# Fixed buffer turns, stores in halves, and a start in half chunks for a matrix product with a decayed running sum

## The chip, the cores and the metric

The kernel runs on one core of a Trainium2 chip. The metric is device time in microseconds (us) of one execution. Times of a kernel are medians of several executions. The profile shows one execution; its span leaves out some 2 us of that execution's time (957.6 of 959.52 us in before).

Engines: TensorE (PE) multiplies, VectorE (DVE) scans and transposes, ScalarE (ACT) reads PSUM and scales, GpSimd (POOL) adds and issues loads, SyncE (SP) issues stores.

## The reference

```python
# x: 16 x 2048 x 1024, w: 1024 x 1024, decay: 1024, all fp32
xw = x @ w
out[:, 0, :] = xw[:, 0, :]
for t in range(1, S):
    out[:, t, :] = decay[None, :] * out[:, t - 1, :] + xw[:, t, :]
```

## The kernel before

The sequence is cut into 64 chunks of 512 steps. GpSimd loads a chunk of x as bf16, VectorE transposes it ("turn"), and VectorE or ScalarE copies it into the layout for the product ("part"). The result comes in eight column tiles n = 0 to 7 of 128 channels. Most of the time two chunks form a group, and a column tile of a group fills two PSUM banks. A few groups have one chunk; there two column tiles share a two-bank PSUM tile. Of chunk 0, the first six column tiles (the "heads") are multiplied side by side while w arrives. Cut, comment added:

```python
groups = ([[0], [1, 2], [3]] + [[c, c + 1] for c in range(4, nch - 2, 2)]
          + [[nch - 2], [nch - 1]])
...
if len(g) == 2:
    ps = psp.tile([128, T], FP32, name="ps")        # pool of 3
else:
    if gi == 0 and n < 6:
        both = heads[n // 2]
    elif n % 2 == 0:
        both = psp.tile([128, 2, TL], FP32, name="ps")
    ps = both[:, n % 2]
```

A column tile is scanned in one of two ways. A *direct* one is scanned by VectorE from PSUM, over all steps. A *paired* one is read by ScalarE (a copy and a scaled copy of every second step), GpSimd adds the two, and VectorE scans only half as many elements; ScalarE and GpSimd then fill in the other half. VectorE transposes each result back into an output tile, which SyncE stores, in the last chunk together with ScalarE:

```python
def store(self, n0, n1):
    for q in (0, 2, 1, 3):
        queue = nc.scalar if self.final and q >= 2 else nc.sync
        queue.dma_start(out=..., in_=self.ot[quad(q), :, n0 * P:n1 * P])
```

Nearly every instruction is wrapped in `pin(...)`, which holds it behind the earlier ones of its own engine. The stores are not. A compiler pass places what is free.

## Time and profile before

| | before |
|---|---|
| median | 961.5 us |
| span of the profile | 957.6 us |
| TensorE busy | 93% |
| matmuls of 512 columns | 4096 |
| first matmul starts | 15.5 us |
| last matmul ends | 939.1 us |
| last transpose ends | 941.6 us |
| last store lands | 956.7 us |

The page gives a span, busy shares, and rows of 40 slices with a digit for tenths; PEclk is the clock that TensorE was granted, in tenths of full speed. The timeline gives, for each run of like instructions, the start, the length, the engine, the line of the kernel, the operation, the operands, the count, and in brackets the idle time before it and what ended it. The lines themselves are in the prediction.

### The profile page before, as it was taken

What the parts mean: (1) busy time and instruction counts of PE and PEld (TensorE: products, weight loads), DVE (VectorE), ACT (ScalarE), POOL (GpSimd) and SP (SyncE); (2) the same over time, 40 slices, a digit from 0 to 9 for tenths busy, and PEclk for the clock granted to TensorE, in tenths of its full rate; (3) what the DMA queues carried; (4) which work ended last, traced back from release to release, by engine and by line L of the source; (5) the groups of instructions that cost most, each with busy time, mean ns of one, the idle gap of its engine ahead of it and who ended that gap; (6) DMA issues with size and microseconds to landing.
All of it is one profiled execution on the core that took longest, in us unless ns stands there. A gap on an engine that the chain in (4) does not pass through costs nothing.

```text
span 957.6 us, 11691 instructions
## 1 busy us (share of the span) xinstructions
PE 891.8 (93%) x4096; PEld 401.9 (42%) x4096; DVE 828.7 (87%) x617; ACT 687.5 (72%) x969; POOL 662.5 (69%) x768
## 2 busy tenths in 40 slices
PE   3497999999999999999999999999999999999871
PEld 1143444444444444444444444444444444444330
DVE  2579799999999999999999999999999999998872
ACT  2567778777877787787778777877777787776630
POOL 7657677777777777777777777767777776765520
PEclk9699999999999999999999999999999999999997
DMA  9998999999999999999999999999999999995917
GB/s 154 152 169 145 257 177 239 222 232 233 231 220 228 231 218 236 235 235 219 230 220 224 239 231 237 224 226 220 227 235 228 237 226 228 222 228 148 236 55 175
DMA packets 278715, 204.20 MB, mean 213 GB/s; under 512 B 7808, under 2 KB 278144, under 8 KB 278656
## 3 DMA queue, kind: packets, MB, share of 16 engines
q1 hardware_dynamic: 140608, 133.18, 54.9%
q0 software_dynamic: 135936, 69.22, 53.1%
q10 hardware_dynamic: 2112, 1.05, 0.5%
q8 instruction: 32, 0.52, 0.2%
q14 instruction: 27, 0.22, 0.1%
HBM read 138.42 MB, written 134.22 MB: 285 GB/s over the span
## 4 chain that ended last, share of the span: by engine, by line
PE 88%; POOL 3%; issue 2%; DVE 2%; DMA 1%; ACT 1%; DVEq 0%; ACTq 0%; POOLq 0%
PE ps L133 88%; POOL xb L105 1%; DMA xb<-in_x_dram 1%; DVE so L194 1%; DVE ot L214 1%; POOL ot L88 1%; POOL xs L179 0%; ACT xs L173 0%; DVE so L185 0%; ACT h L163 0%; POOL so L207 0%; DVE xw L113 0%; ACT xt L121 0%; DVEq L355 0%; POOL so L176 0%
## 5 line engine op out<-in xcount | busy, mean ns | idle before, releaser
L133 PE MATMUL ps<-xt,wsb 128*128 128x512 bf16 x4096 | 891.8, 381 | 47.4 <-ACT h L163 26.1
L133 PEld LDWEIGHTS <-wsb 128*128 128x128 bf16 x4096 | 401.9, 98 | 536.8 <-issue 42.8
L179 POOL TENSOR_TENSOR xs<-h,xs 128x512 f32<-128x512 f32 (+1 forms) x198 | 246.6, 1246 | 221.4 <-ACT h L163 100.8
L173 ACT COPY xs<-ps 128x1024 f32<-128x1024 f32 (+1 forms) x198 | 193.1, 975 | 179.6 <-PE ps L133 178.0
L214 DVE STREAM_TRANSPOSE ot<-so 128x1024 f32<-128x1024 f32 (+1 forms) x272 | 304.3, 1154 | 2.4 <-POOL so L207 1.0
L207 POOL TENSOR_TENSOR so<-h,xs 128x512 f32<-128x512 f32 (+1 forms) x198 | 245.4, 1240 | 29.0 <-ACT h L163 16.1
L121 ACT COPY xt<-xw 128x2048 bf16<-128x2048 bf16 x126 | 239.7, 1902 | 19.3 <-DVE xw L113 19.3
L105 POOL DMA_DIRECT2D xb<-in_x_dram x256 | 170.3, 666 | 2.0 <-DVE xw L113 1.1
L163 ACT ACTIVATE h<-so,dec 128x512 f32<-128x512 f32 (+1 forms) x198 | 148.9, 752 | 27.0 <-DVE so L185 23.2
L185 DVE TENSOR_TENSOR_SCAN so<-dec,keep,xs 128x512 f32<-128x512 f32 (+1 forms) x102 | 124.3, 1218 | 41.3 <-POOL xs L179 41.0
L113 DVE STREAM_TRANSPOSE xw<-xb 128x2048 f32<-128x2048 f32 x64 | 146.3, 2286 | 9.9 <-DMA xb<-in_x_dram 9.9
L185 DVE TENSOR_TENSOR_SCAN so<-dec,xs 128x512 f32<-128x512 f32 (+1 forms) x96 | 114.4, 1191 | 40.5 <-POOL xs L179 37.2
L163 ACT ACTIVATE h<-ps,dec 128x512 f32<-128x512 f32 (+1 forms) x198 | 133.2, 673 | 0.0
L194 DVE TENSOR_TENSOR_SCAN so<-dec,keep,ps 128x1024 f32<-128x1024 f32 (+1 forms) x42 | 84.8, 2019 | 5.4 <-PE ps L133 4.6
L194 DVE TENSOR_TENSOR_SCAN so<-dec,ps 128x1024 f32<-128x1024 f32 (+1 forms) x32 | 70.2, 2194 | 1.7 <-PE ps L133 1.7
L210 ACT COPY keep<-so 128x1 f32<-128x1 f32 x144 | 26.9, 187 | 1.6 <-DVE so L194 1.6
L178 ACT COPY so<-keep 128x1 f32<-128x1 f32 x102 | 19.5, 191 | 0.0
L88 POOL DMA_DIRECT2D ot<-in_w_dram x16 | 8.8, 552 | 4.8 <-DMA xb<-in_x_dram 4.2
L176 POOL MEMSET so<- 128x1 f32 x96 | 11.2, 117 | 0.0
L245 DVE COPY wsb<-ot 128x1024 bf16<-128x1024 bf16 x6 | 2.6, 462 | 4.4 <-DMA ot<-in_w_dram 4.4
L239 DVE TENSOR_TENSOR dec<-dec 128x8 f32<-128x8 f32 x1 | 0.2, 176 | 7.1 <-DMA dec<-in_decay_dram 7.1
L245 ACT COPY wsb<-ot 128x1024 bf16<-128x1024 bf16 x2 | 2.1, 1045 | 4.7 <-DMA ot<-in_w_dram 4.7
(6 smaller groups left out, 4.1 us busy)
## 6 DMA issues: line engine op xcount, KB each, us to landing
out_dram<-ot SPq DMA_DIRECT2D x116, 1024.0 KB, 15.4
xb<-in_x_dram POOLq DMA_DIRECT2D x256, 256.0 KB, 10.0
out_dram<-ot SPq DMA_DIRECT2D x16, 512.0 KB, 8.0
out_dram<-ot SPq DMA_DIRECT2D x12, 256.0 KB, 4.1
ot<-in_w_dram POOLq DMA_DIRECT2D x16, 128.0 KB, 4.8
out_dram<-ot ACTq DMA_DIRECT2D x4, 256.0 KB, 3.5
dec<-in_decay_dram SPq DMA_DIRECT2D x4, 1.0 KB, 3.1
```

Of the source, the lines that this page charges most:

```text
L105: pin(nc.gpsimd.dma_start(out=xb_of[c][quad(q)], in_=_ap(x, [[D, P], [P * D, NJ], [1, CQ]], (b * S + t0) * D + q * CQ)))
L113: pin(nc.vector.transpose(out=dst.rearrange("p (m j i) -> p j m i", m=M, i=P), in_=src.rearrange("p (j m c) -> p j m c", m=M, c=P)))
L121: pin(copy(out=xt_of[c][:, m0:m1], in_=xw_of[c][:, m0:m1].rearrange("p m t e -> p m e t")))
L133: pin(nc.tensor.matmul(out=ps, lhsT=wsb[:, k, n].rearrange("p q i -> p (q i)"), rhs=xt[:, k // 2, k % 2], start=(k == 0), stop=(k == K - 1),))
L163: pin(nc.scalar.activation(out=h, in_=src, func=mybir.ActivationFunctionType.Copy, scale=dec[:, self.n:self.n + 1]))
L173: pin(nc.scalar.copy(out=self.xs, in_=self.ps))
L179: pin(nc.gpsimd.tensor_tensor(out=self.xs[:, 1:T:2], in0=g, in1=self.xs[:, 1:T:2], op=ALU.add))
L185: pin(nc.vector.tensor_tensor_scan(out=so[:, 3:T + 2:2], data0=dec2[:, n:n + 1].to_broadcast([128, T // 2]), data1=self.xs[:, 1:T:2], init ...
L194: pin(nc.vector.tensor_tensor_scan(out=so[:, 2:T + 2], data0=dec[:, n:n + 1].to_broadcast([128, T]), data1=self.ps, initial=0.0 if self.pr ...
L207: pin(nc.gpsimd.tensor_tensor(out=so[:, 2:T + 2:2], in0=h, in1=self.xs[:, 0:T:2], op=ALU.add))
L210: pin(nc.scalar.copy(out=self.keep, in_=so[:, T + 1:T + 2]))
L214: pin(nc.vector.transpose(out=self.ot[:, :, n * P:(n + 1) * P], in_=self.so[:, 2:T + 2].rearrange("p (i t) -> p i t", t=P)))
```

## The change

Its intent: buffers are named and taken in a fixed turn, not from a pool; stores are pinned, and each group goes out in halves of four column tiles; the first two chunks enter in half chunks, with TensorE fed zeros meanwhile so that its clock is up, and the heads are seven. The order of the groups changes too ([0], [1], then pairs), and so does the set of paired tiles in one-chunk groups. Core of the diff, cuts marked, some comments added:

```diff
-    PAIRED = (0, 1, 2, 4, 5, 6)
+    HEADS = 7
+    def ring(pool, name, count, shape, dtype=FP32):
+        i = turns[name] = turns.get(name, -1) + 1
+        return pool.tile(shape, dtype, name=f"{name}{i % count}")
...
-    groups = ([[0], [1, 2], [3]] + [[c, c + 1] for c in range(4, nch - 2, 2)]
+    groups = ([[0], [1]] + [[c, c + 1] for c in range(2, nch - 2, 2)]
               + [[nch - 2], [nch - 1]])
...
+            if len(g) == 2:
+                self.paired = n % 4 != 3
+            else:
+                self.paired = n % 2 == 0 and not (self.final and n == K - 2)
...
-            if self.halved:
-                if n == K // 2 - 1:
-                    self.store(0, K // 2)
-                elif n == K - 1:
-                    self.store(K // 2, K)
-            elif n == K - 1:
-                self.store(0, K)
+            if n == 3:
+                self.store(0, 4)
+            elif n == 5 and self.final:
+                self.store(4, 6)
+            elif n == 7:
+                self.store(6 if self.final else 4, 8)
...
-                queue.dma_start(
+                pin(queue.dma_start(
...
+    for _ in range(40):
+        pin(nc.tensor.matmul(out=spare, lhsT=idle[:, 0:128], rhs=idle, start=True, stop=True))
+    H = NJ // 2
+    for j0 in (0, H):
+        for q in range(NQ):
+            load(0, q, j0, j0 + H)
...
+    at(1, turn, 1, 0, H)                      # chunk 1: first half behind tile 1 of chunk 0
+    at(1, part, 1, nc.vector.tensor_copy, 0, 2, 0, H)
+    at(1, part, 1, nc.scalar.copy, 2, M, 0, H)
+    at(3, turn_last_half, 1)                  # second half behind tile 3
...
+        elif gi == 1:                         # chunk 1's first four tiles, in halves
+            bank = [ring(psp, "ps", 3, [128, 2, TL]) for _ in range(2)]
+            heads = [bank[n // 2][:, n % 2] for n in range(4)]
+            for t0 in (0, H * P):
+                for n in range(4):
+                    for k in range(K):
+                        matmul(heads[n], n, k, xt_of[1], t0, t0 + H * P)
```

More of the change, by code (lines that the diff above doesn't have):

```diff
@@ L59 @@
     NC = S // TL
-    PAIRED = (0, 1, 2, 4, 5, 6)
+    HEADS = 7
     const = ctx.enter_context(tc.tile_pool(name="const", bufs=1))
-    xbp = ctx.enter_context(tc.tile_pool(name="xbp", bufs=3))
-    xwp = ctx.enter_context(tc.tile_pool(name="xwp", bufs=2))
-    xtp = ctx.enter_context(tc.tile_pool(name="xtp", bufs=5))
-    sop = ctx.enter_context(tc.tile_pool(name="sop", bufs=4))
-    tmp = ctx.enter_context(tc.tile_pool(name="tmp", bufs=2))
-    otp = ctx.enter_context(tc.tile_pool(name="otp", bufs=2))
@@ L69 @@
-    psp = ctx.enter_context(tc.tile_pool(name="psp", bufs=3, space=bass.MemoryType.PSUM))
-    pdp = ctx.enter_context(tc.tile_pool(name="pdp", bufs=1, space=bass.MemoryType.PSUM))
+    sb = ctx.enter_context(tc.tile_pool(name="sb", bufs=1))
+    psp = ctx.enter_context(tc.tile_pool(name="psp", bufs=1, space=bass.MemoryType.PSUM))
+    turns = {}
+    def ring(pool, name, count, shape, dtype=FP32):
+        i = turns[name] = turns.get(name, -1) + 1
+        return pool.tile(shape, dtype, name=f"{name}{i % count}")
@@ L72, in quad @@
     def quad(q):
         return slice(q * P, (q + 1) * P)
-    dec = const.tile([128, K], FP32, name="dec")
-    dec2 = pdp.tile([128, 512], FP32, name="dec2")
-    wsb = const.tile([128, K, K, NQ, P], BF16, name="wsb")
-    with nc.allow_non_contiguous_dma(reason="a vector of 1024"):
-        for q in range(NQ):
-            nc.sync.dma_start(
-                out=dec[quad(q), :], in_=_ap(decay, [[1, P], [P, K]], q * CQ))
-    def load_w():
-        wb = otp.tile([128, M, 2 * D], BF16, name="ot")
-        for m in range(M):
-            for q in range(NQ):
-                pin(nc.gpsimd.dma_start(
-                    out=wb[quad(q), m],
-                    in_=_ap(w, [[2 * D, P], [1, 2 * D]], (q * CQ + m * 2 * P) * D)))
-        return wb.rearrange("p m (e q n i) -> p (m e) q n i", e=2, q=NQ, n=K)
@@ L93 @@
     chunks = [(b, c * TL) for b in range(B) for c in range(NC)]
     nch = len(chunks)
-    xt_of = {}
-    xw_of = {}
-    xb_of = {}
-    def load(c, q):
-        if c >= nch:
-            return
-        b, t0 = chunks[c]
-        if q == 0:
-            xb_of[c] = xbp.tile([128, NJ, CQ], BF16, name="xb")
-        pin(nc.gpsimd.dma_start(
-            out=xb_of[c][quad(q)],
-            in_=_ap(x, [[D, P], [P * D, NJ], [1, CQ]], (b * S + t0) * D + q * CQ)))
-    def turn(c):
-        xw = xwp.tile([128, M, TL, 2], BF16, name="xw")
-        src = xb_of.pop(c).rearrange("p j c -> p (j c)").bitcast(FP32)
-        dst = xw.rearrange("p m t e -> p (m t e)").bitcast(FP32)
-        pin(nc.vector.transpose(
-            out=dst.rearrange("p (m j i) -> p j m i", m=M, i=P),
-            in_=src.rearrange("p (j m c) -> p j m c", m=M, c=P)))
-        xw_of[c] = xw
@@ L118, in part @@
-    def part(c, copy, m0, m1):
-        if m0 == 0:
-            xt_of[c] = xtp.tile([128, M, 2, TL], BF16, name="xt")
-        pin(copy(
-            out=xt_of[c][:, m0:m1],
-            in_=xw_of[c][:, m0:m1].rearrange("p m t e -> p m e t")))
-    groups = ([[0], [1, 2], [3]] + [[c, c + 1] for c in range(4, nch - 2, 2)]
+    groups = ([[0], [1]] + [[c, c + 1] for c in range(2, nch - 2, 2)]
               + [[nch - 2], [nch - 1]])
@@ L128, with ot_tile, load, turn @@
         assert chunks[g[0]][0] == chunks[g[-1]][0]
-    last = {}
-    def matmul(ps, n, k, xt):
+    dec = const.tile([128, K], FP32, name="dec")
+    dec2 = psp.tile([128, 512], FP32, name="dec2")
+    spare = psp.tile([128, TL], FP32, name="spare")
+    wsb = const.tile([128, K, K, NQ, P], BF16, name="wsb")
+    def ot_tile():
+        return ring(sb, "ot", 2, [128, 2 * NJ, CQ])
+    xb_of = {}
+    xw_of = {}
+    xt_of = {}
+    def load(c, q, j0=0, j1=NJ):
+        b, t0 = chunks[c]
+        if c not in xb_of:
+            xb_of[c] = ring(sb, "xb", 3, [128, NJ, CQ], BF16)
+        pin(nc.gpsimd.dma_start(
+            out=xb_of[c][quad(q), j0:j1],
+            in_=_ap(x, [[D, P], [P * D, j1 - j0], [1, CQ]],
+                    (b * S + t0 + j0 * P) * D + q * CQ)))
+    def turn(c, j0=0, j1=NJ):
+        if c not in xw_of:
+            xw_of[c] = ring(sb, "xw", 2, [128, M, NJ, P, 2], BF16)
+        src = xb_of[c][:, j0:j1].rearrange("p j c -> p (j c)").bitcast(FP32)
+        dst = xw_of[c].rearrange("p m j i e -> p (m j i e)").bitcast(FP32)
+        pin(nc.vector.transpose(
+            out=dst.rearrange("p (m j i) -> p j m i", m=M, i=P)[:, j0:j1],
+            in_=src.rearrange("p (j m c) -> p j m c", m=M, c=P)))
+    def part(c, copy, m0, m1, j0=0, j1=NJ):
+        if c not in xt_of:
+            xt_of[c] = ring(sb, "xt", 5, [128, M, 2, TL], BF16)
+        src = xw_of[c][:, m0:m1, j0:j1].rearrange("p m j i e -> p m e (j i)")
+        pin(copy(out=xt_of[c][:, m0:m1, :, j0 * P:j1 * P], in_=src))
+    def matmul(ps, n, k, xt, t0=0, t1=TL):
         pin(nc.tensor.matmul(
-            out=ps,
+            out=ps[:, t0:t1],
             lhsT=wsb[:, k, n].rearrange("p q i -> p (q i)"),
-            rhs=xt[:, k // 2, k % 2],
+            rhs=xt[:, k // 2, k % 2, t0:t1],
             start=(k == 0),
@@ L139, in matmul @@
         ))
+    last = {}
     class Tile:
@@ L150, in __init__ @@
             self.final = gi + 1 == len(groups)
-            self.halved = gi + 3 >= len(groups)
-            self.paired = n in PAIRED and not self.final
-            self.so = sop.tile([128, self.T + 2], FP32, name="so")
+            if len(g) == 2:
+                self.paired = n % 4 != 3
+            else:
+                self.paired = n % 2 == 0 and not (self.final and n == K - 2)
+            self.so = ring(sb, "so", 4, [128, 2 * TL + 2])
             self.prev = None if self.t0 == 0 else last[n]
@@ L161, in decayed @@
         def decayed(self, src):
-            h = tmp.tile([128, self.T // 2], FP32, name="h", bufs=4)
+            h = ring(sb, "h", 4, [128, TL])[:, 0:self.T // 2]
             pin(nc.scalar.activation(
@@ L171, in pair @@
             T = self.T
-            self.xs = tmp.tile([128, T], FP32, name="xs", bufs=3)
+            self.xs = ring(sb, "xs", 3, [128, 2 * TL])[:, 0:T]
             pin(nc.scalar.copy(out=self.xs, in_=self.ps))
@@ L227, in store @@
                 queue = nc.scalar if self.final and q >= 2 else nc.sync
-                queue.dma_start(
+                pin(queue.dma_start(
                     out=_ap(out, [[D, P], [P * D, self.T // P], [1, (n1 - n0) * P]],
                             (self.b * S + self.t0) * D + q * CQ + n0 * P),
-                    in_=self.ot[quad(q), :, n0 * P:n1 * P])
-    for q in range(NQ):
-        load(0, q)
-    wv = load_w()
-    for c in range(1, 3):
-        for q in range(NQ):
-            load(c, q)
+                    in_=self.ot[quad(q), :, n0 * P:n1 * P]))
@@ new lines @@
+    with nc.allow_non_contiguous_dma(reason="a vector of 1024"):
+        for q in range(NQ):
+            nc.sync.dma_start(
+                out=dec[quad(q), :], in_=_ap(decay, [[1, P], [P, K]], q * CQ))
+    idle = const.tile([128, TL], BF16, name="idle")
+    pin(nc.vector.memset(idle, 0.0))
+    for _ in range(40):
+        pin(nc.tensor.matmul(out=spare, lhsT=idle[:, 0:128], rhs=idle, start=True, stop=True))
+    H = NJ // 2
+    for j0 in (0, H):
+        for q in range(NQ):
+            load(0, q, j0, j0 + H)
@@ new lines @@
+    wb = ot_tile().rearrange("p j c -> p (j c)")[:, 0:M * D].bitcast(BF16)
+    wm = wb.rearrange("p (m d) -> p m d", m=M)
+    for m in range(M):
+        for q in range(NQ):
+            pin(nc.gpsimd.dma_start(
+                out=wm[quad(q), m],
+                in_=_ap(w, [[2 * D, P], [1, 2 * D]], (q * CQ + m * 2 * P) * D)))
+    for j0 in (0, H):
+        for q in range(NQ):
+            load(1, q, j0, j0 + H)
+    for q in range(NQ):
+        load(2, q)
+    for j0 in (0, H):
+        turn(0, j0, j0 + H)
+        part(0, nc.vector.tensor_copy, 0, 2, j0, j0 + H)
+        part(0, nc.scalar.copy, 2, M, j0, j0 + H)
@@ L239 @@
     pin(nc.vector.tensor_tensor(out=dec2[:, 0:K], in0=dec, in1=dec, op=ALU.mult))
-    turn(0)
-    part(0, nc.vector.tensor_copy, 0, 2)
-    part(0, nc.scalar.copy, 2, M)
+    wk = wb.rearrange("p (k q n i) -> p k q n i", k=K, q=NQ, n=K)
     for k in range(K):
         copy = nc.scalar.copy if k % 4 == 3 else nc.vector.tensor_copy
-        pin(copy(out=wsb[:, k].rearrange("p n q i -> p q n i"), in_=wv[:, k]))
+        pin(copy(out=wsb[:, k].rearrange("p n q i -> p q n i"), in_=wk[:, k]))
+    agenda = {}
@@ L246, with at @@
     loads = []
-    agenda = {}
-    def prepare(c, l, first):
-        def turned():
-            turn(c)
-            loads.extend((c + 3, q) for q in range(NQ))
-        ahead = (7, 6, 4) if l else (11, 10, 8)
-        steps = (turned, lambda: part(c, nc.scalar.copy, 0, 2),
-                 lambda: part(c, nc.scalar.copy, 2, M))
-        for a, f in zip(ahead, steps):
-            agenda.setdefault(first - a, []).append(f)
+    def at(step, f, *args):
+        agenda.setdefault(step, []).append(lambda: f(*args))
@@ L261, with turn_and_load, turn_last_half @@
+    def turn_and_load(c):
+        turn(c)
+        if c + 3 < nch:
+            loads.extend((c + 3, q) for q in range(NQ))
+    def turn_last_half(c):
+        turn(c, H, NJ)
+        loads.extend((c + 3, q) for q in range(NQ))
+    at(1, turn, 1, 0, H)
+    at(1, part, 1, nc.vector.tensor_copy, 0, 2, 0, H)
+    at(1, part, 1, nc.scalar.copy, 2, M, 0, H)
+    at(3, turn_last_half, 1)
+    at(3, part, 1, nc.vector.tensor_copy, 0, 2, H, NJ)
+    at(3, part, 1, nc.scalar.copy, 2, M, H, NJ)
     for gi, g in enumerate(groups):
@@ L263 @@
             if c > 1:
-                prepare(c, l if len(g) == 2 else 1, gi * K)
-    loads.extend((3, q) for q in range(NQ))
-    turn(1)
-    loads.extend((4, q) for q in range(NQ))
-    part(1, nc.vector.tensor_copy, 0, 2)
-    part(1, nc.scalar.copy, 2, M)
-    def feed(step):
-        for f in agenda.pop(step, []):
-            f()
-        for _ in range(2 if len(loads) > NQ else 1):
-            if loads:
-                load(*loads.pop(0))
+                first = gi * K
+                ahead = (7, 6, 4) if l or len(g) == 1 else (11, 10, 8)
+                at(first - ahead[0], turn_and_load, c)
+                at(first - ahead[1], part, c, nc.scalar.copy, 0, 2)
+                at(first - ahead[2], part, c, nc.scalar.copy, 2, M)
     waiting = []
@@ L297, in behind @@
                 tl.back()
+    loads.extend((3, q) for q in range(NQ))
     for gi, g in enumerate(groups):
@@ L301 @@
         if len(g) == 2:
-            ot = otp.tile([128, T // P, CQ], FP32, name="ot")
+            ot = ot_tile()
         else:
             if g[0] in (0, nch - 2):
-                halves = otp.tile([128, 2 * TL // P, CQ], FP32, name="ot")
+                halves = ot_tile()
             ot = halves[:, g[0] % 2 * NJ:(g[0] % 2 + 1) * NJ]
-        xts = [xt_of.pop(c) for c in g]
+        heads = []
         if gi == 0:
-            heads = [psp.tile([128, 2, TL], FP32, name="ps") for _ in range(3)]
+            bank = [ring(psp, "ps", 3, [128, 2, TL]) for _ in range(3)]
+            heads = [bank[n // 2][:, n % 2] for n in range(6)] + [spare]
@@ L310 @@
             for k in range(K):
-                for n in range(6):
-                    matmul(heads[n // 2][:, n % 2], n, k, xts[0])
+                for n in range(HEADS):
+                    matmul(heads[n], n, k, xt_of[0])
+        elif gi == 1:
[5 more added lines that the diff above has]
+                        matmul(heads[n], n, k, xt_of[1], t0, t0 + H * P)
@@ L313 @@
         for n in range(K):
-            if len(g) == 2:
-                ps = psp.tile([128, T], FP32, name="ps")
-            else:
-                if gi == 0 and n < 6:
-                    both = heads[n // 2]
-                elif n % 2 == 0:
-                    both = psp.tile([128, 2, TL], FP32, name="ps")
-                ps = both[:, n % 2]
-            if gi > 0 or n >= 6:
+            if n < len(heads):
+                ps = heads[n]
+            else:
+                if len(g) == 2:
+                    ps = ring(psp, "ps", 3, [128, T])
+                elif gi == 0:
+                    ps = ring(psp, "ps", 3, [128, 2, TL])[:, 0]
+                else:
+                    if n % 2 == 0:
+                        both = ring(psp, "ps", 3, [128, 2, TL])
+                    ps = both[:, n % 2]
@@ L323 @@
                 for k in range(K):
-                    for l in range(len(g)):
-                        matmul(ps[:, l * TL:(l + 1) * TL], n, k, xts[l])
+                    for l, c in enumerate(g):
+                        matmul(ps[:, l * TL:(l + 1) * TL], n, k, xt_of[c])
             behind(Tile(gi, n, ps, ot))
-            feed(gi * K + n)
+            for f in agenda.pop(gi * K + n, []):
+                f()
+            for _ in range(2 if len(loads) > NQ else 1):
+                if loads:
+                    load(*loads.pop(0))
```

## The prediction

> **What bounds the kernel now.** I read the page's slices first, then the chain that ended last, then the timeline of TensorE at both ends.
>
> ```profile
> PE   3497999999999999999999999999999999999871
> PEclk9699999999999999999999999999999999999997
> 95.41 799.62 PE ps L133 x3704
> ```
>
> The third line is a piece of the chain: start, length, what. For 800 us the chain is nothing but matmuls, 799.62 / 3704 = 0.2159 us each. All 4096 would take 884.3 us; the span is 957.6, so 73 us can be won, and only before 95 us and after 898 us. The timeline of TensorE there (start, length, and in brackets the idle time before and who ended it):
>
> ```profile
> 15.47 12.13 PE L133 MATMUL ps<-xt,wsb 128*128 128x512 bf16 x48 [15.47 <-DVE wsb L245]
> 33.69 3.57 PE L133 MATMUL ps<-xt,wsb 128*128 128x512 bf16 x8 [6.09 <-ACT h L163]
> 45.35 33.26 PE L133 MATMUL ps<-xt,wsb 128*128 128x512 bf16 x144 [8.09 <-ACT h L163]
> ...
> 901.25 3.61 PE L133 MATMUL ps<-xt,wsb 128*128 128x512 bf16 x16 [1.05 <-ACT h L163]
> 907.09 3.61 PE L133 MATMUL ps<-xt,wsb 128*128 128x512 bf16 x16 [2.22 <-ACT h L163]
> ...
> 922.04 3.61 PE L133 MATMUL ps<-xt,wsb 128*128 128x512 bf16 x16 [1.48 <-DVE so L194]
> ...
> 937.23 1.89 PE L133 MATMUL ps<-xt,wsb 128*128 128x512 bf16 x8 [1.41 <-DVE so L194]
> ```
>
> **Start.** At 95.41 us TensorE has done 248 matmuls, worth 53.5 us: 41.9 us lost. 15.5 is data; 6.1 and 8.1 follow; 2.3 goes in the clock, since matmuls come 0.43 us apart at 15.5 and 45.4; the four stops of the one-chunk group [3] cost 6.
>
> **One-chunk groups.** Every stop lies ahead of an odd column tile n: n and n-1 share a two-bank PSUM tile, and the odd half is not written until the even half has been read (n=0 of chunk 62 ends at 900.2, ScalarE reads it until 901.2, n=1 starts at 901.25).
>
> **End.** VectorE ends at 941.6, the span at 957.6. SyncE's queue says why (total wait, times, longest):
>
> ```profile
> SPq L228 <- DMA out_dram<-ot: 32.2, 4, 25.2
> ```
>
> The instruction list shows the stores of chunk 62, ready at about 913 and 922, issued at 935.9 and later. They wait for semaphores that the last chunk's stores on ScalarE's queue had been given first (issued 932.79 and 941.66). The scheduler was free to order the stores. SyncE's last eight stores then go out 944.7 to 951.7, the last landing at 956.7.
>
> **What the Trainium skill says.**
> 1. "TensorE: Matmul & The Clock Gate", Part 1 (the HAM clock gate): an idle array runs at half rate, returns to full after a busy window of about 3.4 us, and falls back after an idle one. The trace agrees: 0.43 against 0.216 us, full rate 3.3 us after 15.47, and half rate again from 32.4.
> 2. "DMA: Bandwidth & Descriptors", Specifications: pieces under 512 B pay a read-modify-write. Stores of halves have 512 B rows, the last four column tiles of the last chunk 256 B rows. The trace has 512 B: queue q1 was busy 92.3% of 16 engines over 904 to 911 us with 3374 packets, 30.6 ns each; the 1 KB packets of 400 to 500 us took 59.2% with 14929, 63.4 ns each. So halves cost the same per byte. No 256 B store is in the trace.
>
> **The change, part by part.**
>
> *Fixed rotation:* in the steady 800 us nothing waits but TensorE, which stopped once. 0 us.
>
> *Stores in halves:* twice the stores, same transfer time (above). 0 us in the middle.
>
> *Spin-up:* 40 matmuls of zeros from about 1 us: some 12 at 0.43 and 28 at 0.216, done by about 12, before data. Half chunks let VectorE turn the first half while the second lands (chunk 0 all landed at 11.4, w in pieces from 13.9 to 21.4, the same bytes in the same order): half turn 1.15 + half copy 0.62 ends at 13.3, then the first piece of w, copied at 14.4, instead of 15.47. With seven heads 56 matmuls take 12.1: TensorE is done at 26.5 (before: 48 at 27.4). One us earlier, eight matmuls more: worth 2.6 us.
>
> *Then the start is bound by VectorE and ScalarE, in fixed order.* Per two column tiles of 512, VectorE does a paired scan 0.62, a direct scan 1.12, two transposes 1.24 (start to start in the trace): 2.98. A turn of a chunk is 2.2. ScalarE needs 1.0 to read a paired tile, POOL 0.7 to add; half of a chunk's copy takes ScalarE 1.9. The timelines of these engines show it (the next start gives the step):
>
> ```profile
> 38.39 0.69 DVE L185 TENSOR_TENSOR_SCAN so<-dec,xs 128x256 f32<-128x256 f32 x1 [0.69 <-POOL xs L179]
> 39.00 1.19 DVE L194 TENSOR_TENSOR_SCAN so<-dec,ps 128x512 f32<-128x512 f32 x1
> 40.11 0.68 DVE L214 STREAM_TRANSPOSE ot<-so 128x512 f32<-128x512 f32 x1
> ...
> 40.88 1.90 ACT L121 COPY xt<-xw 128x2048 bf16<-128x2048 bf16 x1
> 42.68 0.59 ACT L173 COPY xs<-ps 128x512 f32<-128x512 f32 x1
> 43.16 0.49 ACT L163 ACTIVATE h<-ps,dec 128x256 f32<-128x256 f32 x1
> ```
>  Following the program's order on each queue, since nearly every instruction is held to it:
> - n=0 is read by 26.4, POOL adds by 27.2, scans 0 and 1 end at 28.95: n=7 of chunk 0 may then use their banks, 28.95 to 30.7.
> - half turn and copy of chunk 1, ScalarE's copy to 31.15, read of n=2 to 32.1, add 32.8, scans 2 and 3 to 34.6: chunk 1's n=0,1 start on half data.
> - the second half turn and copy to 36.4, read of n=4 37.8, scans 4 and 5 to 40.3: n=2,3 start, and the second half runs to about 45.6.
> - turn of chunk 2 to 42.5; scans 6, 7 to 45.5: n=4 of chunk 1 from 45.6 to 47.3.
> - n=5 needs n=4 read. ScalarE first does two chunk copies (to 47.9), reads n=2, waits for chunk 3's turn (50.7), copies (52.6): n=4 read at 54.2.
> - after 7 us idle the clock is low: n=5 to 57.7, n=6 to 60.3, read 61.3, n=7 to 63.1.
>
> Pairs start at 63.1 with 128 matmuls (27.6 us) done: 35.5 lost, against 41.9. **Start gains 6.4 us.**
>
> *Chunk 62:* n=3 still waits for ScalarE, which waits for VectorE's backlog of 1024-wide transposes and the turn of chunk 63; redoing the list gives n=7 at 917.15 against 916.94 (old clock). 0 us.
>
> *Last chunk:* even tiles are now read by ScalarE in 1.05 instead of VectorE's 1.28 plus what lies ahead of it: a step of two tiles goes from 5.09 to 4.7, three times; n=6 stays direct. VectorE's last transpose ends near 940.6 instead of 941.6. Gain 1.0.
>
> *Last stores:* issued in program order, chunk 62's are out of the way by 930. The last eight (n=4,5 and n=6,7) are 512 packets of 256 B each. I take 30 ns a packet as for 512 B: 0.96 us each over 16 engines. The first four are issued at 937.4, start 1.9 later and end at 943.3; the last four follow to 947.2. The drain after the last landing is 0.95: 948.1 against 957.6. **The end gains 9.5 us, the 1.0 included.**
>
> Sum: 6.4 + 9.5 = 15.9; a little off because the list above leaves out the 20 to 50 ns between a release and the next start, some 30 times on the chain over both ends, and part of that is in the durations: 15.5. Median 961.8 - 15.5 = **946.3 us**.
>
> **Rivals.**
> 1. *The wait moves, not goes, at the start.* If ScalarE's copies hold n=4's read longer, or the clock falls in the idle stretches at 31 and 36 too, the start gains nothing. For: I count 20 us idle of TensorE after 26.5, all by in-order queues. Against: the old start had the same kind of waits, plus the group [3]. Time: 952.
> 2. *The 256 B stores pay the read-modify-write and take 60 ns.* Eight of them take 15.4 us: the end comes near 956, the gain there is 2. For: the skill's line. Against: nothing else is in flight by then. Time: 954.
> 3. *The odd half no longer waits for the even one.* If the new buffers are tracked by bank, n=5 starts at 47 and the tail's stops vanish: 8 us and some 6 more. For: fixed names change how buffers are released. Against: the wait is inside one tile, where the code is as before. Time: 933.
> 4. *The smaller stores crowd the loads in the middle.* The two queues have 59.2% and 56.8% and share the same engines ("DMA: Bandwidth & Descriptors", Issuing engines are not separate DMA queues). Twice as many packets could delay a load. Against: loads are issued some 20 us ahead and land in 10. Time: 955 to 965.
>
> **Range and chances.** The end's 9.5 rests on a wait that the trace shows and on packets that it doesn't (7 to 11); the start's 6.4 on a list of 30 steps (1 to 12). Together 8 to 23: 939 to 954. Faster by over 2% means below 942.5: it needs a start near 10, or rival 3: 0.28. Slower by over 2% needs rival 4 in the extreme: 0.01. Within 2%: 0.71.
>
> **What would show it.** Right: first real matmul near 14.4 and 0.216 apart at once; 56 of them by 26.5; the longest stop after that ahead of chunk 1's n=5, about 7 us, ended by ScalarE; pairs from 63; stops of about 1.1 at odd n in the last chunk; stores of chunk 62 issued before the last chunk's; last landing some 6 to 7 us after the last transpose. Wrong: no stop ahead of odd n (rival 3); last landing over 10 us after the last transpose (rival 2); matmuls of the middle spaced over 0.2165 (rival 4); pairs starting after 68 (rival 1).

## The result, and the profile after

The kernel after takes 955.31 us (954.45 to 957.45, 4 runs) against 961.46 us in the same rounds: ratio 0.9943, interval 0.9921 to 0.9966. The change gains some 6 us, or 0.6%, and I had said 15.5. 955.3 lies outside my range of 939 to 954.

| | before | after | gained |
|---|---|---|---|
| span of the profile | 957.6 | 953.6 | 4.0 |
| groups of two chunks end on TensorE | 898.5 | 895.1 | 3.4 |
| from there to the last transpose | 43.1 | 41.9 | 1.2 |
| from the last transpose to the last landing | 15.0 | 15.7 | -0.7 |
| from the last landing to the end | 0.9 | 0.9 | 0 |

The rows from the second on add to 3.9, the span's 4.0 but for rounding. The two profiles don't stand at the same place among their kernels' runs: before's execution took 959.52 us, 1.6 to 2.5 below the three runs timed with it (961.15 to 962.04), and after's 955.39 lies in the middle of its four. So the table has some 2 us less than the medians' 6; where these 2 us lie, no kept trace shows. The middle gave and took nothing. The slices of the page after, TensorE's busy share and its granted clock:

```profile
PE   8669999999999999999999999999999999999871
PEclk9789999999999999999999999999999999999997
```

TensorE is full from the fourth slice on, 72 us; in before it was from the fifth. The start is the timeline of TensorE after; the first line is the run of zeros:

```profile
1.20 10.29 PE L234 MATMUL spare<-idle 128*128 128x512 bf16 x40 [1.20 <-DVE idle L232]
14.20 2.50 PE L123 MATMUL ps<-xt,wsb 128*128 128x512 bf16 x6 [2.71 <-DVE wsb L259]
...
30.76 2.83 PE L123 MATMUL ps<-xt,wsb 128*128 128x512 bf16 x8 [2.62 <-DVE so L188]
36.48 3.57 PE L123 MATMUL ps<-xt,wsb 128*128 128x256 bf16 x16 [2.89 <-DVE so L188]
42.20 8.58 PE L123 MATMUL ps<-xt,wsb 128*128 128x256 bf16 x56 [2.15 <-DVE so L188]
57.37 6.02 PE L123 MATMUL ps<-xt,wsb 128*128 128x512 bf16 x16 [6.59 <-ACT h L157]
64.44 45.92 PE L123 MATMUL ps<-xt,wsb 128*128 128x512 bf16 x212 [1.05 <-ACT h L157]
```

These are the stops of my list, in its order: n=7 of chunk 0, n=0,1 and n=2,3 of chunk 1 on half data, n=5, n=7. But the six matmuls from 14.20 on took 2.50 us, where later runs of six took 1.46. Two stretches of the windows view of after (the stretch, its length, busy time and count of PE, PEld, DVE, ACT and POOL, the granted clock, DMA share, GB/s) show the clock:

```profile
11.50:14.20 2.70, 0.00 (x1) 0.01 (x1) 2.20 (x5) 1.04 (x1) 2.36 (x5) 1.00 1.06 208
14.20:17.90 3.70, 3.70 (x10) 1.39 (x11) 0.70 (x2) 1.04 (x1) 3.23 (x7) 0.54 1.04 204
```

The zeros had ended at 11.49, the clock fell to half at 14.49 and came back at 17.90. So the clock was up when the zeros ended, and with the gap of 2.7 us behind them it fell again.

The end is read from SyncE's queue, first its waits (total, times, longest, from 880 us on), then its timeline:

```profile
SPq L221 <- DMA out_dram<-ot: 31.6, 4, 25.8
```

```profile
901.54 3.08 SPq L221 DMA_DIRECT2D out_dram<-ot  x3
...
930.46 19.79 SPq L221 DMA_DIRECT2D out_dram<-ot  x15
```

The wait of before is still there, no shorter (25.8 against 25.2 us). The queue stands still from 904.6 to 930.46, though chunk 62's halves are ready near 910 and 918; then 15 stores go out one behind the other: the fourth of the last pair's second half, eight of chunk 62, six of the last chunk. From 915 to 930 the DMA engines did next to nothing, and much of what was left undone is made up for behind the last transpose at 936.98 (windows view of after; the same columns):

```profile
915.00:930.00 15.00, 11.85 (x55) 5.11 (x53) 10.24 (x14) 5.40 (x15) 4.57 (x7) 1.00 0.10 20
930.00:938.00 8.00, 3.10 (x14) 1.14 (x12) 5.82 (x7) 0.00 (x0) 0.57 (x1) 1.00 0.92 190
938.00:954.00 16.00, 0.00 (x0) 0.00 (x0) 0.00 (x0) 0.00 (x0) 0.00 (x0) 0.55 0.83 183
```

The instruction list names the semaphore. SyncE's store at 930.46, the last pair's, waits for semaphore 109; chunk 62's stand behind it, from 931.93 on. ScalarE's first store of the last chunk, issued at 927.44, counts on 109 and landed at 930.44. So an older store waits for a younger one on another queue. The wrapper `pin` fixes the order on one engine. It says nothing about which of two engines is given a semaphore first, and that is what held the stores in before.

### The profile page after: what moved, and what is told of

It is laid out like the page before. It is cut to its first block, busy times and chain, and to the rows that moved or that the text cites. A ratio compares the mean times of both kernels' runs of the same rounds, so it can differ in the third digit from the quotient of the medians.

```text
span 953.6 us, 12026 instructions
## 1 busy us (share of the span) xinstructions
PE 904.8 (95%) x4168; PEld 410.6 (43%) x4168; DVE 830.6 (87%) x622; ACT 684.9 (72%) x961; POOL 663.1 (70%) x768
## 3 DMA queue, kind: packets, MB, share of 16 engines
q10 hardware_dynamic: 3168, 1.05, 0.6%
## 5 line engine op out<-in xcount | busy, mean ns | idle before, releaser
L123 PE MATMUL ps<-xt,wsb 128*128 128x512 bf16 (+1 forms) x4120 | 893.8, 380 | 28.4 <-ACT h L157 16.7
L123 PEld LDWEIGHTS <-wsb 128*128 128x128 bf16 x4128 | 406.4, 98 | 516.6 <-issue 36.0
L167 ACT COPY xs<-ps 128x1024 f32<-128x1024 f32 (+1 forms) x194 | 190.4, 982 | 186.1 <-PE ps L123 183.1
L120 ACT COPY xt<-xw 128x2048 bf16<-128x2048 bf16 (+1 forms) x128 | 240.1, 1876 | 17.6 <-DVE xw L112 17.6
L102 POOL DMA_DIRECT2D xb<-in_x_dram x264 | 174.8, 663 | 7.9 <-DVE xw L112 6.0
L112 DVE STREAM_TRANSPOSE xw<-xb 128x2048 f32<-128x2048 f32 (+1 forms) x66 | 146.6, 2221 | 8.1 <-DMA xb<-in_x_dram 8.1
L188 DVE TENSOR_TENSOR_SCAN so<-dec,ps 128x1024 f32<-128x1024 f32 (+1 forms) x34 | 72.6, 2135 | 0.0
L234 PE MATMUL spare<-idle 128*128 128x512 bf16 x40 | 10.3, 424 | 1.2 <-DVE idle L232 1.2
L234 PEld LDWEIGHTS <-idle 128*128 128x128 bf16 x40 | 4.2, 108 | 6.8 <-issue 1.9
```

The costliest lines, as they stand in the source:

```text
L102: pin(nc.gpsimd.dma_start(out=xb_of[c][quad(q), j0:j1], in_=_ap(x, [[D, P], [P * D, j1 - j0], [1, CQ]], (b * S + t0 + j0 * P) * D + q * CQ)))
L112: pin(nc.vector.transpose(out=dst.rearrange("p (m j i) -> p j m i", m=M, i=P)[:, j0:j1], in_=src.rearrange("p (j m c) -> p j m c", m=M, c=P)))
L120: pin(copy(out=xt_of[c][:, m0:m1, :, j0 * P:j1 * P], in_=src))
L123: pin(nc.tensor.matmul(out=ps[:, t0:t1], lhsT=wsb[:, k, n].rearrange("p q i -> p (q i)"), rhs=xt[:, k // 2, k % 2, t0:t1], start=(k == 0), ...
L167: pin(nc.scalar.copy(out=self.xs, in_=self.ps))
L188: pin(nc.vector.tensor_tensor_scan(out=so[:, 2:T + 2], data0=dec[:, n:n + 1].to_broadcast([128, T]), data1=self.ps, initial=0.0 if self.pr ...
```

## The experiments

My theory of the lost gain has two parts. **(T1)** The end gained nothing because stores on two queues still share one set of semaphores. **(T2)** The start gained half of what I said because the clock fell behind the spin-up. The rivals: the end is bound by how fast the stores drain, or by rows of 256 B; the start by the fixed order of VectorE and ScalarE whatever the clock does. All 12 runs gave a correct result, and each was timed in 5 rounds against before. "After" below means the kernel after.

### One queue for the last stores

```diff
-                queue = nc.scalar if self.final and q >= 2 else nc.sync
+                queue = nc.sync
```

> The kernel after, with all stores of the last chunk on SyncE's queue instead of half of them on ScalarE's. My theory: the end lost its gain because the stores of the two queues still share DMA semaphores, and a store of the last chunk on ScalarE's queue was given a semaphore before older stores on SyncE's, so those wait for it from 905 to 930 us. With one queue the order is fixed: stores of chunk 62 issued near 908 and 918, the last eight right behind VectorE's last transposes, the last landing 6 to 7 us after the last transpose (937.0 in the profile after) instead of 15.7: the span falls from 953.6 to about 945, by 8 to 9 us. Rival, that the end is bound by how fast the stores drain (21 stores in 22 us) or by pieces of 256 B: under 2 us change.

Measured: 942.98 us (before 961.32, ratio 0.9812, interval 0.9798 to 0.9827), which is 12.3 us better than after, more than expected. The waits of SyncE and the same stretches as above, now of this run:

```profile
SPq L221 <- DVE ot L208: 32.0, 7, 8.0
```

```profile
905.00:915.00 10.00, 7.37 (x34) 3.22 (x33) 8.62 (x12) 7.02 (x14) 2.96 (x4) 1.00 0.95 229
915.00:930.00 15.00, 11.85 (x55) 5.15 (x53) 10.24 (x14) 5.39 (x15) 4.41 (x6) 1.00 0.50 117
938.00:954.00 16.00, 0.00 (x0) 0.00 (x0) 0.00 (x0) 0.00 (x0) 0.00 (x0) 0.86 0.17 33
```

SyncE's stores no longer wait for a transfer at all, only for VectorE to finish tiles. Chunk 62's stores are issued from 910.3 and 918.3; TensorE and VectorE do the same as in after (last transpose 937.15 against 936.98), and the last landing follows the last transpose by 4.0 us, not 15.7. T1 holds, and the drain as a rival falls: with the same bytes, the end is 11.5 us earlier in the profile.

### A second queue with semaphores of its own

```diff
-                queue = nc.scalar if self.final and q >= 2 else nc.sync
+                queue = nc.gpsimd if self.final and q >= 2 else nc.sync
```

> The kernel after with half of the last chunk's stores on GpSimd's queue instead of ScalarE's: still two queues, but in the trace GpSimd's transfers count on semaphores 99 to 106 and those of SyncE and ScalarE together on another eight. Theory: what holds chunk 62's stores back is the semaphore shared across the two queues, not a second queue as such: with GpSimd they go out near 908 and 918 as with one queue, and the median is 942 to 945. Rival, that any second queue for the last chunk lets the older stores on SyncE be ordered behind it: 953 or more.

Measured: 944.03 us (before 961.73, ratio 0.9821, interval 0.9808 to 0.9835). SyncE's stores of chunk 62 go out from 908.2 and 916.1. So a second queue is not the fault as such. GpSimd's queue differs in more than its semaphores (352 packets for its 1.05 MB of stores, where ScalarE's has 3168), so this run alone doesn't single out the semaphores; the store that waits for 109 in after does.

### One queue in the kernel before

The same edit as the first, in before.

> The kernel before with all stores of the last chunk on SyncE's queue, nothing else. My theory: the same wait was in before, the stores of chunk 62 then go out near 913 and 922 and the last landing is about 7 us after the last transpose at 941.6: span 949 to 950 instead of 957.6, which is what I had predicted of the change itself. Rival, that pinning the order is needed as well, since the scheduler may place stores freely even on one queue: no change, or under 3 us.

Measured: 952.53 us (ratio 0.9909, interval 0.9895 to 0.9923): 8.8 us off, with not a word of the change. Pinning was not needed. (The profile is of the fastest run, 950.12; the other four took 952.28 to 953.28.) SyncE's longest wait is 6.2 us, for VectorE, and the last landing at 947.4 comes 6.2 us behind the issue of the last four stores.

### Own PSUM tiles in one-chunk groups

```diff
-                    if n % 2 == 0:
-                        both = ring(psp, "ps", 3, [128, 2, TL])
-                    ps = both[:, n % 2]
+                    ps = ring(psp, "ps", 3, [128, 2, TL])[:, 0]
```

> The kernel after, with each column tile of a one-chunk group in a PSUM tile of its own (half of it unused) instead of two in one tile. My theory: the waits ahead of odd n are waits inside one tile for the even half to be read. They vanish: ahead of n=5 of chunk 1 (6.6 us) and n=7 (1.05) at the start, and the eight of 1.05 to 2.2 us at the end (10.4 us in sum). At the start n=5 can begin as soon as n=0 and n=1 have been read, near 51 instead of 57.4, but n=6 waits for n=2 and n=3 (57): 3 to 5 us. At the end TensorE finishes 6 to 9 us earlier, but the stores still wait as in after, so the last landing gains less than that or nothing beyond what the order of the stores lets through. Span 940 to 948. Rival, that VectorE binds in the one-chunk groups: TensorE waits for it instead, under 3 us.

Measured: 950.64 us (ratio 0.9891, interval 0.9877 to 0.9904), 4.7 better than after. Its timeline of TensorE, the start and the end:

```profile
51.34 1.89 PE L123 MATMUL ps<-xt,wsb 128*128 128x512 bf16 x8 [0.35 <-DVE so L188]
57.20 13.04 PE L123 MATMUL ps<-xt,wsb 128*128 128x512 bf16 x48 [3.97 <-DVE so L188]
...
900.37 3.61 PE L123 MATMUL ps<-xt,wsb 128*128 128x512 bf16 x16 [1.34 <-DVE so L188]
905.56 17.43 PE L123 MATMUL ps<-xt,wsb 128*128 128x512 bf16 x80 [1.58 <-DVE so L188]
```

n=5 of chunk 1 starts at 51.34, not 57.37; then n=6 waits for older tiles to be read, as foreseen. At the end eight stops became two. The last 80 matmuls run through, and VectorE ends near 927.3 instead of 937.0. The span fell by 4.6 us only, to 949.0, where I had expected 940 to 948: the stores still waited, and the last landing came 20.9 us behind the last transpose. So the stops ahead of odd n do come from sharing one PSUM tile. My third rival had hoped that the change itself would end them; it didn't.

### Both

> Both edits that worked alone: all stores on SyncE's queue, and a PSUM tile of its own for each column tile of the one-chunk groups. My theory: the own tiles made VectorE end at 927.3 instead of 937.0, but the span fell by 4.6 only because the stores still waited; with one queue the last landing follows the last transpose by 4.0 us, so the span is about 932.5 and the median 933 to 934: the gains of the two (12.3 and 4.7) add to more than their sum, 21 to 22 us against after. Rival, that the stores of the last two chunks, 4.2 MB, drain no faster than some 230 GB/s from 905 on: the last landing is 2 to 4 us later, median 936.

Measured: 931.91 us (before 960.82, ratio 0.9702, interval 0.9689 to 0.9714). It beats before by 3.0% and after by 23.4 us, where the single edits gave 12.3 and 4.7. That is a little more than the 21 to 22 us that I had expected, and the rival's 936 falls. The last landing follows the last transpose by 4.6 us. Two waits in a row hide each other: each edit alone is worth less than it is beside the other.

### Both, in the kernel before

> The kernel before with both edits that worked: stores of the last chunk on SyncE's queue, own PSUM tiles for the column tiles of one-chunk groups. It shows what the change itself is worth once these two waits are gone (against 931.91 of the kernel after with both). Theory: one queue gave before 9 us; own tiles take away the stops ahead of odd n, 8.1 us at n=7 of chunk 0 in part, some 4 of the 6 in the group [3], and up to 11 at the end, where VectorE then binds because the last chunk is scanned directly: median 938 to 943. The change's own parts would then be worth 6 to 11 us. Rival, that the change is worth nothing beyond these waits: 932 to 934.

The edit of the PSUM tiles, in the words of before:

```diff
-                elif n % 2 == 0:
-                    both = psp.tile([128, 2, TL], FP32, name="ps")
-                ps = both[:, n % 2]
+                    ps = both[:, n % 2]
+                else:
+                    ps = psp.tile([128, 2, TL], FP32, name="ps")[:, 0]
```

Measured: 937.30 us (before 960.11, ratio 0.9755, interval 0.9742 to 0.9768). Against the ratio 0.9702 of the run above, the change's own parts are worth 0.53% of 960 us, about 5 us, once both waits are gone; I had expected 6 to 11. The two small edits do more in either kernel than the whole change.

### A longer spin-up, and none

```diff
-    for _ in range(40):
+    for _ in range(52):      # and in another run range(0)
```

> The kernel after with 52 matmuls of zeros instead of 40, to close the gap of 2.7 us ahead of the first real matmul, in which the granted clock fell to half from 14.49 to 17.90. My theory: the real matmuls of chunk 0 then come 0.216 us apart from the first on, the seven heads end near 26.5 instead of 28.1, and all that follows at the start moves by it: pairs start 1.5 to 2 us earlier, span 951.5 to 952. Rival, that VectorE and ScalarE bind the start and take the 1.6 us up: within 0.5 us of after. If the clock rises later in the run, the spin-up ends later than 14.2 and eats up to 1.5 of it.

> The kernel after without any matmul of zeros. Theory: as the clock fell anyway ahead of the first real matmul in after (half rate from 14.49 to 17.90), the spin-up as it stands gives nothing: within 1 us of after (955.3). Rival, that it gives the 1 to 3 us it was made for: 957 or more.

Measured: 955.49 us with 52 (ratio 0.9937, interval 0.9923 to 0.9950), 955.82 us with none (ratio 0.9950, interval 0.9938 to 0.9962), against 955.31 of after. With 52 the gap closes and the clock stays up to 29.86; n=7 of chunk 0 starts at 29.64 instead of 30.76. But the zeros now end at 14.94 and hold the first real matmul back to 14.77, and the clock falls in the later stops (half rate from 29.86 to 33.28 and from 36.69 to 46.93), so n=5 of chunk 1 starts at 57.64, no earlier than in after. So I was wrong that the 1.6 us of the heads would last. With none, the first matmuls are slow up to 18.69, as in after up to 17.90, and every stop lies within 0.7 us of after's. The medians of after with and without the spin-up don't differ by what these runs can tell.

I overlooked that whether it works is a matter of luck. In the profiles with 40 zeros the clock first rises at 4.25 to 5.93 us, so the zeros end at 11.49 to 12.33; the first real matmul comes at 13.56 to 14.58 (15.55 with whole chunks, below). The gap between them differs accordingly. In five profiles (after among them) the gap was 2.52 to 3.78 us and the clock fell; in three it was 1.48 to 1.91 and the clock stayed up. The kernel with one queue and the one with whole stores below, which start alike, each have two runs at 941.8 to 942.2 us and two at 943.8 to 944.0. The profile of the first kernel is a slower run (943.88), where the clock fell; that of the second kernel is a faster one (941.93), where it stayed up, and n=5 of chunk 1 starts 2.0 us earlier. So a kept clock seems to be worth some 2 us, though one profile of each shows it. It also means that medians of four runs can differ by 1 us by this alone.

> As the kernel with one queue and own tiles, and 52 matmuls of zeros instead of 40. With 52 the seven heads ended earlier but the clock then fell during the later idle stretches and nothing was left at the end of the start. Theory: the start is bound by VectorE's and ScalarE's order and a falling clock, so within 1 us of the kernel with 40. Rival, that the loss behind the heads in the run with 52 was chance of the clock's phase: 1.5 us faster.

Measured: 933.61 us (ratio 0.9717, interval 0.9704 to 0.9730) against 931.91 with 40: 1.7 us slower, with intervals that overlap. The theory had said within 1 us, the rival 1.5 us faster. In the profile of the kernel with 40 the clock had stayed up (gap 1.91 us), so there was little to win. The longer spin-up is no help; whether it hurts stays open.

### Whole chunks at the start

The kernel with one queue; chunks 0 and 1 are loaded, turned and copied whole, and chunk 1's first four tiles are not cut.

```diff
-    at(1, turn, 1, 0, H)
-    at(1, part, 1, nc.vector.tensor_copy, 0, 2, 0, H)
-    at(1, part, 1, nc.scalar.copy, 2, M, 0, H)
-    at(3, turn_last_half, 1)
-    at(3, part, 1, nc.vector.tensor_copy, 0, 2, H, NJ)
-    at(3, part, 1, nc.scalar.copy, 2, M, H, NJ)
+    at(1, turn_and_load, 1)
+    at(1, part, 1, nc.vector.tensor_copy, 0, 2)
+    at(1, part, 1, nc.scalar.copy, 2, M)
...
```

> The kernel with one queue (942.98), but chunks 0 and 1 are loaded, turned and copied whole, as before, and chunk 1's first four tiles are not cut into halves; seven heads, order of groups, spin-up and stores stay. Theory: the first real matmul comes at 15.5 instead of 14.2, and chunk 1's tiles n=0,1 wait for a whole turn and copy, but VectorE's order is bound by its sum of work, which is the same but for some 0.3 us per cut: pairs start 1 to 3 us later, median 944 to 946. Rival, that the halves are what the start's gain of 3.4 us comes from: 946.5 or more. Second rival, that cutting costs as much as it gives: within 1 us.

Measured: 945.64 us (ratio 0.9847, interval 0.9833 to 0.9860) against 942.98: the halves are worth 2.7 us in the medians. The profiles don't show all of it. The first real matmul comes at 15.55, and n=7 of chunk 1 at 65.34 (64.63 in the profile with halves): 0.7 us. Another 1.2 us went in chunk 62, where the clock fell once for n=3 and n=4 (5.30 us for 16 matmuls instead of 3.61); the run with 52 zeros has the same fall there, so it may be a matter of when the stops come. Against the two slower runs of the kernel with one queue (943.78 and 943.88), of which the profile is one, the median is 1.8 us up, about what the two profiles show (1.9); the rest of the 2.7 is its two faster runs, where the clock probably stayed up. Here the gap was 3.78 us and all four runs lie within 0.8. What the halves save by earlier data alone is thus 0.7 us in the profiles.

### Whole stores in the middle

The kernel with one queue; groups of two chunks stored whole, as in before.

```diff
+            whole = self.T == 2 * TL
-            if n == 3:
+            if n == 3 and not whole:
                 self.store(0, 4)
...
-                self.store(6 if self.final else 4, 8)
+                self.store(0 if whole else 6 if self.final else 4, 8)
```

> The kernel with one queue, but the groups of two chunks stored whole as before, 1 MB for each quadrant in rows of 1 KB. Theory: halves and wholes cost the same in the middle, where nothing waits for a store: TensorE's 0.2159 us per matmul stays. At the end the last pair's 4.2 MB go out 14 us later at once and lie ahead of chunk 62's stores on the queue; they land by 916 as in before, so the last landing moves by under 1 us. Median within 1 us of 943.0. Rival, halves themselves help (a buffer that comes free sooner) or hurt (twice as many packets): over 2 us.

Measured: 942.92 us (ratio 0.9816, interval 0.9802 to 0.9830) against 942.98. Halves in the middle are worth nothing, as said. The start of its profile, one of the faster runs, is used below (the second line is n=5 of chunk 1):

```profile
13.80 1.47 PE L123 MATMUL ps<-xt,wsb 128*128 128x512 bf16 x6 [1.48 <-DVE wsb L260]
...
55.46 6.11 PE L123 MATMUL ps<-xt,wsb 128*128 128x512 bf16 x16 [6.58 <-ACT h L157]
```

One point of the expectation was off: the last pair's stores landed until 922.1, not 916, and chunk 62's behind them, but the last landing did not mind.

### Two last pieces instead of three

The kernel with one queue; the last chunk stored as tiles 0 to 3 and 4 to 7.

```diff
-            elif n == 5 and self.final:
-                self.store(4, 6)
             elif n == 7:
-                self.store(6 if self.final else 4, 8)
+                self.store(4, 8)
```

> The kernel with one queue (942.98), but the last chunk stored in two pieces of four column tiles (rows of 512 B) instead of pieces of four, two and two (rows of 256 B). With one queue the last landing came 4.0 us after the last transpose with the last four stores of 128 KB, and in the kernel before with one queue 6.2 us after it with four of 256 KB. Theory: small last pieces help, since bytes still to be moved at the end halve and 256 B rows pay nothing visible: this one is 2 us slower, 945. Rival, the one I had feared in the prediction, that 256 B rows cost twice the time per packet: this one is equal or faster.

Measured: 946.20 us (ratio 0.9850, interval 0.9836 to 0.9863) against 942.98; the last landing follows the last transpose by 6.4 us, not 4.0. The small pieces help by 2.4 us in the profile. The packets tell why. In the run with three pieces the DMA view gives, for 927.6 to 933.9 us (rows of 512 B) and for 934 to 942 us (rows of 256 B), packets, MB and the share of 16 engines:

```profile
q1 hardware_dynamic: 2112, 1.05, 70.1%
...
q1 hardware_dynamic: 4224, 1.05, 67.0%
```

0.701 x 16 x 6.3 us / 2112 = 33.5 ns, and 0.670 x 16 x 8 us / 4224 = 20.3 ns. A row of half the size takes 0.6 of the time, where I had put in the same time and feared the double.

## Why the prediction was wrong

By its steps:

- **The middle, rotation and halves: 0 us.** Right. TensorE ran through from 64.44 to 895, and whole stores in the same place changed nothing (942.92 against 942.98).
- **The last chunk: 1.0 us.** Right: 1.2.
- **Chunk 62: 0 us.** Right: its stops of 1.05, 2.23, 1.58 and 1.05 us are those of before, 1.05, 2.22, 1.53 and 1.10.
- **The last stores: this is the step that failed.** "Issued in program order, chunk 62's are out of the way by 930." They weren't issued before 931.93, and came after two of the last chunk's; SyncE's longest wait for a transfer was 25.8 us, where it had been 25.2. I had found the right wait in before, a semaphore that a younger store on ScalarE's queue holds, and then took the pinning for its cure. Pinning orders one engine's instructions; the wait is between two engines. Taking away the second queue gave what I had credited to the change and more: 12.3 us in after, 8.8 in before. My figure for a working end was 948.1 on the old clock; with the wait gone it would have been too careful still, since 256 B packets took 20.3 ns, not 30.
- **Spin-up and heads: 2.6 us, with the first real matmul at 14.4 and the heads done by 26.5.** The first matmul came at 14.20, the heads ended at 28.1. I had the end of the zeros at 12 (11.49) and did not ask what a gap of two to three microseconds does to the clock. In the profile of the kernel with one queue and own tiles the zeros happened to end closer to the first real matmul (gap 1.91 us), the clock stayed up, and there my list holds within 0.5 us: n=7 at 28.44 (28.95 predicted), n=0,1 at 34.17 (34.6), n=2,3 at 39.89 (40.3).
- **The start's 6.4 us.** The mechanism held, the size didn't: 3.4. Pairs started at 66.2 instead of 63.1. Of the 3.1 us, 1.8 to 1.9 are there at each stop from 30.76 to 42.20, from the clock at the heads, and 3.2 at n=5 (57.37 against 54.2). The profile of the kernel with whole stores, whose start is that of after, tells the two apart, since there the clock stayed up behind the zeros (gap 1.48 us): n=2,3 at 40.13 (40.3 predicted), n=5 at 55.46 (54.2), n=7 at 62.62 (61.3). So the clock took 1.9 us, and my list of the queues between 40 and 55 us was 1.3 short: there ScalarE's copy of chunk 3 starts at 51.41 (50.7), and before it reads n=4 ScalarE waits another 0.64 us for a scan of VectorE's, which the list lacks.
- **The account of the old start.** The total of 41.9 us lost is right, its parts are not: those listed add to 38.0, and the clock cost more than 2.3. At half rate TensorE multiplied from 15.47 to 18.73, 33.69 to 37.26 and 45.35 to 49.45, 10.9 us, of which half is lost, 5.5. Nor does every stop lie ahead of an odd n: that of 6.09 us lies ahead of n=6 of chunk 0. Neither went into the sum.
- **The rivals.** The first (the wait moves at the start) was as far off as I: the start gained 3.4, it had said 0 and I 6.4. Both things that it named were seen, the later read of n=4 and the clock falling at 31. The second fell: its sign, a last landing over 10 us behind the last transpose, did come (15.7), but from the semaphore, and the packets took 20.3 ns, not 60. The third fell for the change, though its edit, done by hand, works. The fourth fell.
- **The chances.** "Within 2%" at 0.71 was the outcome; the range was too tight at its upper end, because I took the end's gain for the part that a trace had shown.

## What to carry to other kernels

When a wait on a semaphore goes across two queues, a fixed order on each queue doesn't remove it. Look up which instruction counts the semaphore up, and move that one to a queue that doesn't share it. And where two waits lie in a row before the end, undo both before judging either: here 12.3 and 4.7 us alone made 23.4 together.

## What the Trainium skill lacked or had wrong

- "DMA: Bandwidth & Descriptors", Issuing engines are not separate DMA queues, says that a second issuing engine saves only issue time. In these runs it cost 12.3 us (955.31 against 942.98), as the program has its transfers and those of the first engine count on one set of semaphores, and at most some 1 us when the second engine had another set (944.03). No page that I found says that an older store can be held by a younger one of another engine in this way.
- The same page, Specifications, puts rows under 512 B at a read-modify-write, without a cost. In the runs a 256 B packet took 20.3 ns and a 512 B packet 33.5 ns, some 1.2 times as long per byte, and small last pieces ended 2.4 us earlier. Whether there was a read-modify-write no run shows.
- "TensorE: Matmul & The Clock Gate", Part 1, lets the clock fall after an idle window of about 3.4 us. Here shorter stops were enough: it fell behind the zeros with 2.52 us without a matmul (the kernel with one queue) and 2.71 (after: zeros ended 11.49, real ones from 14.20, half rate from 14.49), and not with 1.91. The length alone doesn't decide: a stop of 2.23 us in chunk 62 let it fall in two profiles (52 zeros; whole chunks) and not in after. In each trace the clock's changes lie 3.41 us or a multiple apart.
- "PSUM — Partial Sum Buffer", Summary, advises to read a bank other than the one that matmuls write. The halves of a shared tile are such banks, but that was not enough: here the program held a matmul into one half until the other half had been read, eight times in the last two chunks, 10.4 us in all. With a tile for each, two stops were left, 2.9 us.
